# A hybrid diffusion block on one core: the two halves of the retention's gate columns issued ahead of the query convolution instead of behind it

## The chip, the cores and the metric

The kernel runs on one core of one Trainium2 chip. The metric is the device time of one execution in microseconds (us), and a kernel's time is the median of several runs.

## The reference, cut to what matters

One layer of a diffusion backbone with 1024 latent and 256 context tokens of width 1024. One input projection `p = h @ w_in` is split by columns between two groups of four heads. Group A is a gated delta rule (GDN) in both directions, with a centred convolution of five taps on its q, k and v columns. Group B is retention in both directions, with a rotary embedding on q and k, and a gate `rg`:

```
qkv_a, z, ab, rq, rk, rv, rg = jnp.split(p, splits, axis=-1)
qkv_a = concat([short_conv(ctx part, cw), short_conv(latent part, cw)])   # taps, then silu
q, k, v = heads of qkv_a;  q = l2_normalize(q) * HEAD_DIM**-0.5;  k = l2_normalize(k)
...
A   = strict_lower((k * beta) @ k.T * decay)       # per chunk and head
sol = triangular_solve(A + I, [v * beta, k * beta * exp(G)])
qk  = (q @ k.T) * decay
...
o_gdn = rms_norm(o_f + o_b, gdn_norm_g) * silu(z)
o_ret = head_group_norm(r_f + r_b, ret_norm_g) * silu(rg)
y = concat([o_gdn, o_ret])
```

Then follow the output projection, a gated residual, a SwiGLU and a final norm. The columns `rg` are used only in the product `silu(rg)` with the retention's output, long after the part in which they are computed.

## The kernel before

Tokens lie in 10 tiles of 128, tiles 0 and 1 being the context. Products run in two-part fp32: each operand is split into a high part, a copy on ScalarE (L344), and the rest, on VectorE or GpSimd (L345), and three matmuls stand for one.

Two kinds of products fill the stretch around the change. `token_major(g, ...)` computes 256 columns of the projection for a list of tiles, with tokens on partitions: per tile 8 x 3 matmuls of 128x256 (L371 to L373) into a PSUM bank `tm`, a finishing step into `res`, and a store. For the gates (g = 6 and 7, latent tiles alone) that step is a Silu on ScalarE (L532), and the store to DRAM goes out on ScalarE's queue (L387). `conv_block(b, y, lat)` computes one head of 128 columns with channels on partitions, 8 x 3 matmuls for each of two or three pieces of tokens (L611 to L613) into `b2`. Two copies on ScalarE (u, L614, and y, L615), four taps on VectorE (L621) and a Silu (L624) follow.

The program is written in this order: four key heads, each stored and its norms taken (`kstat`); a logarithm and a reciprocal root of the norms; four query heads, each stored to DRAM as `qd` on ScalarE's queue (L682); the gates; then, for the chunks of a batch, `pre(t)` and `invert(b)`, and four value heads. `BATCH = [[0,1,2,9],[3,8,4,7],[5,6]]` lists the tiles of each batch. `pre(t)` loads the keys `kc` and, for a latent tile, the queries `qc` (both on SP, L664), multiplies keys by keys (kk, L705), transposes the queries (qt, L710) and multiplies them by the keys (kq, L715). For each direction it loads a row of decays into `gw` (L718, two buffers), masks it on GpSimd (e, L722), takes its exponential on ScalarE (L726), multiplies on VectorE (ut, L730, and sp, L732) and stores ut as `un` (L733). The second exponential of gw (L735) is multiplied by the queries on GpSimd (L736), which frees that gw. `invert(b)` loads `un` as yr (L751), inverts blocks of 32 on VectorE in 31 steps (L759, L765, L767) and stores them as `xd` (L771). `merge(b)` loads them again (L787, L788) and joins them on PE (m1, L807 on). The value heads are transposed (vT, L856), scaled on ScalarE into vt (L859, two buffers) and stored as `sd` (L860). The gate columns of z, `token_major` of g = 8 and 9, come behind the merges.

That is the order of the text only. A scheduler places each instruction in the order of its engine by the estimated time at which its inputs are ready, with the place in the text as priority, and at run time each engine keeps the order it was given. So products with nothing to wait for stand between those that wait.

Of the kernel before, what the change touches and what calls it, by code (L numbers as in the profile page):

```python
# [38 lines left out]
def build(nc, tc, ap, dbg=None, stop=None, marks=None):  # L39
    root = ExitStack()  # L40
    V, S, G, T, SY = nc.vector, nc.scalar, nc.gpsimd, nc.tensor, nc.sync

    def pool(name, bufs=1, side=None, space=None):
        kw = {}
        if side is not None:
            kw["side"] = side
        if space is not None:
            kw["space"] = space
        if space is not DRAM:
            kw["reuse_waits"] = "tile"  # L50
        es = ExitStack()
        p = es.enter_context(tc.tile_pool(name=name, bufs=bufs, **kw))
        root.push(es)
        p_close[id(p)] = es
        return p
# [10 lines left out]
    def checkpoint(name):  # L66
        if dbg is not None:
            marks.append((name, int(nc.cur_bb.bb.instructions[-1].name.split("-")[-1])))
        if stop == name:
            raise Stop()  # L70
# [120 lines left out]
    try:  # L191
# [40 lines left out]
        W2 = None  # L232
# [127 lines left out]
        def tm_weights(g, kh, pl, q=S):  # L360
            return weights(ap["wt"][g, :, 4 * kh:4 * kh + 4, :], [4, 256], V, pl, q, raws.get((g, kh)), g == 0)

        def tm_bank(g):
            return bank_a("tm")[:, 0:WIDE if g == 0 else 256]

        def tm_half(o, w, kh, t):

            tsl = slice(t * P, (t + 1) * P)
            whi, wlo = w
            for k in range(4 * kh, 4 * kh + 4):  # L370
                T.matmul(o, hhi[:, k, tsl], whi[:, k % 4, :], start=(k == 0), stop=False)  # L371
                T.matmul(o, hhi[:, k, tsl], wlo[:, k % 4, :], start=False, stop=False)  # L372
                T.matmul(o, hlo[:, k, tsl], whi[:, k % 4, :], start=False, stop=(k == KT - 1))  # L373
# [5 lines left out]
        def tm_store(g, t, o, finish, store, pl):  # L379
            early = g < 2  # L380
            res = (W2 if early else R1).tile([P, 256], F32, tag="res", name="res", bufs=4 if early else 2)
            finish(t, o[:, 0:256], res)
            if g == 0:
                S.activation(xa[:, t, :], o[:, 256:WIDE], AF.Copy)
            nm, c0 = GROUPS[g // 2], (g % 2) * 256
            dst = zd[t - 2, :, c0:c0 + 256] if nm == "z" else rd[t, :, RD[nm], c0:c0 + 256]
            store.dma_start(dst, res)  # L387

        def token_major(g, tiles, finish, store, pl, q=S):

            w = [tm_weights(g, kh, pl, q) for kh in range(2)]

            for p in range(0, len(tiles), 2):
                pair = [(t, tm_bank(g)) for t in tiles[p:p + 2]]
                for kh in range(2):
                    for t, o in pair:
                        tm_half(o, w[kh], kh, t)
                for t, o in pair:
                    tm_store(g, t, o, finish, store, pl)
# [47 lines left out]
        W2 = pool("w2", bufs=2)  # L447
# [39 lines left out]
        def ada_rest(c, half):  # L487

            c0 = c * D + half * 512
            src = ap["ada2"][2 * (c - 2) + half]  # L490
            acc = R2.tile([P, 512], F32, tag="acc", name="acc", bufs=1)
            for k in range(KT):
                if k % 2 == 0:
                    w = R2.tile([P, 2, 512], F32, tag="adaw2", name="adaw2", bufs=2)
                    SY.dma_start(w, src[k // 2])
                if k == 0:
                    V.tensor_scalar(acc, w[:, 0], csl[:, k, 0:1], None, ALU.mult)
                else:
                    V.scalar_tensor_tensor(acc, w[:, k % 2], csl[:, k, 0:1], acc, ALU.mult, ALU.add)
            ps = bank_b("gr")  # L500
            if c in (2, 5):
                row = R2.tile([1, 512], F32, tag="row", name="row", bufs=1)
                SY.dma_start(row, ap["adarow"][c0:c0 + 512].unsqueeze(0))
                T.matmul(ps[:1, :], ones[:, 0:1], acc, start=True, stop=True)
                V.tensor_tensor(row, row, ps[:1, :], ALU.add)
                SY.dma_start(grow[0 if c == 2 else 1][:, half * 512:(half + 1) * 512], row)
            else:
                for k in range(4):
                    T.matmul(ps[:, 2 * k:2 * k + 2], acc[:, k * P:(k + 1) * P], ones[:, 0:2], start=True, stop=True)
                ks = slice(half * 4, half * 4 + 4)  # L510
                o = ada2[:, c - 3, ks]
                V.tensor_tensor(o, ps[:, 0:8].rearrange("p (k t) -> p k t", t=2)[:, :, 0],
                                adab[:, 8 * c + 4 * half:8 * c + 4 * half + 4], ALU.add)
                if c == 4:
                    V.scalar_tensor_tensor(o, o, 1.0, gffn[:, ks], ALU.add, ALU.mult)
# [18 lines left out]
        LAT, ALL = list(range(2, TT)), list(range(2, TT)) + [0, 1]  # L534
# [67 lines left out]
        def conv_block(b, y, lat):  # L602

            whi, wlo = weights(ap["wg"][b], [KT, P], G if b % 2 else V, W, SY if b in (4, 5) else S)
            u = CV.tile([P, NTOK], F32, tag="u", name="u", bufs=2)
            for c0, n in (CHUNKS[1:] if lat else CHUNKS):
                ps = bank_c("b2")
                o = ps[:, :n]
                for k in range(KT):
                    hh, hl = hhi[:, k, c0:c0 + n], hlo[:, k, c0:c0 + n]  # L610
                    T.matmul(o, whi[:, k, :], hh, start=(k == 0), stop=False)  # L611
                    T.matmul(o, whi[:, k, :], hl, start=False, stop=False)  # L612
                    T.matmul(o, wlo[:, k, :], hh, start=False, stop=(k == KT - 1))  # L613
                S.activation(u[:, c0:c0 + n], o, AF.Copy)  # L614
                S.activation(y[:, c0:c0 + n], o, AF.Copy, scale=cw[:, b, 2:3])  # L615
            segs = [(NCTX, NLAT)] if lat else [(0, NCTX), (NCTX, NLAT)]
            for i, e in ((0, V), (1, V), (3, V), (4, V)):
                for s0, n in segs:
                    sh = i - 2
                    lo, hi = s0 + max(0, -sh), s0 + n - max(0, sh)  # L620
                    e.scalar_tensor_tensor(y[:, lo:hi], u[:, lo + sh:hi + sh], cw[:, b, i:i + 1], y[:, lo:hi],  # L621
                                           ALU.mult, ALU.add)
            a0 = NCTX if lat else 0
            S.activation(y[:, a0:], y[:, a0:], AF.Silu)  # L624

        def newy():
            return CV.tile([P, NTOK], F32, tag="y", name="y", bufs=3)
# [46 lines left out]
        sv = rsqrt(GS, nkf, TT * H, "sv")  # L674
        V.tensor_tensor(sv, sv, nkf, ALU.mult)
        sv3 = sv.rearrange("p (t h) -> p t h", h=H)
        for h in range(H):
            y = newy()
            conv_block(h, y, True)
            if h < 2:  # L680
                ada_rest(5, h)
            S.dma_start(qd[:, :, h, :].rearrange("t p j -> p t j"),  # L682
                        y[:, NCTX:].rearrange("p (t j) -> p t j", j=P))

        checkpoint("q")
        for g in (6, 7):
            token_major(g, LAT, fin_gate, S, W2, SY)
        checkpoint("rg")
        close(R2)
        close(W2)  # L690
# [964 lines left out]
```

## Time and profile before

| what | before |
|---|---|
| runs, median (lowest to highest) | 1478.84 us (1476.53 to 1480.8), 3 runs |
| the profiled execution | 1477.96 us, its span 1476.2 us |
| granted TensorE clock, mean | 0.983 |
| PE, weight loads, VectorE, ScalarE, GpSimd busy | 95%, 81%, 65%, 42%, 40% |

Names of engines: PE is TensorE's matmul, DVE is VectorE, ACT ScalarE, POOL GpSimd, SP the engine that issues most loads. A row of a timeline has the start, the duration, the engine, the line, the operation, what it writes from what it reads, and a count; in brackets stands the idle time of that engine ahead of it and what ended it. ACTq and SPq are instructions that issue a DMA. A row of a stretch has its window and its length, then the busy time of PE, PE's weight loads, DVE, ACT and POOL with their counts, the granted clock, the share of the DMA engines and GB/s.

### The profile page before, as it was taken

The page shows a single profiled execution, that of the slowest core. Times are in us where ns is not written, and L with a number is a line of the kernel's source. Part 1 is how long each engine was busy: PE and PEld are TensorE (multiplying, and loading weights), DVE is VectorE, ACT ScalarE, POOL GpSimd, SP SyncE. Part 2 cuts the span into 40 slices and gives each one's busy share as a digit, 9 for nine tenths or more (in the row PEclk, how much of TensorE's full clock was granted, in tenths as well). Part 3 has the DMA queues.
Part 4 walks back from the last instruction along what each step waited for, and adds up shares of the span by engine and source line. Part 5 has one row for each costly group of instructions (what it writes and reads, how often), then busy time and mean ns, then how long its engine had stood idle before and what let it go on. Part 6 is the DMA issues. An engine that isn't in the chain of part 4 may idle for free.

```text
span 1476.2 us, 24111 instructions
## 1 busy us (share of the span) xinstructions
PE 1397.2 (95%) x8919; PEld 1199.2 (81%) x8919; DVE 964.6 (65%) x1856; ACT 614.0 (42%) x1326; POOL 590.3 (40%) x501
## 2 busy tenths in 40 slices
PE   7999999986789999899799899999999999999997
PEld 2898888975689999898688688877888888788885
DVE  6566789289792435689676877556555564657477
ACT  5643564587333111245443623233333332444445
POOL 0120010243202344234144688898555552335321
PEclk9999999998899999999899999999999999999999
DMA  9536686688888625996532265674222242776863
GB/s 337 197 105 205 189 249 200 219 264 277 282 216 277 238 76 178 416 341 209 184 125 104 97 238 210 242 264 162 105 97 105 107 151 79 260 260 194 288 216 114
DMA packets 170421, 298.14 MB, mean 202 GB/s; under 512 B 43496, under 2 KB 93880, under 8 KB 165952
## 3 DMA queue, kind: packets, MB, share of 16 engines
q1 hardware_dynamic: 118752, 253.17, 50.2%
q10 hardware_dynamic: 49072, 35.83, 7.8%
q0 software_dynamic: 2480, 7.60, 1.4%
q8 instruction: 70, 1.15, 0.3%
q14 instruction: 47, 0.39, 0.1%
HBM read 206.60 MB, written 89.96 MB: 201 GB/s over the span
## 4 chain that ended last, share of the span: by engine, by line
PE 55%; POOL 6%; DMA 5%; DVE 4%; issue 2%; ACT 2%; SPq 1%; ACTq 0%; POOLq 0%; DVEq 0%
PE ffn L1344 7%; PE ffn L1342 6%; PE ffn L1343 6%; PE fo L1470 4%; PE fo L1469 4%; PE fo L1468 4%; PE tm L371 3%; PE tm L373 3%; PE tm L372 3%; PE op L1203 2%; PE op L1201 2%; PE op L1202 2%; DMA wd<-tw 2%; POOL ws L1315 1%; DMA pk<-sd 1%
## 5 line engine op out<-in xcount | busy, mean ns | idle before, releaser
L371 PE MATMUL tm<-whi,hhi 128*128 128x256 f32 (+1 forms) x704 | 199.5, 287 | 7.7 <-ACT vt L859 3.4
L372 PE MATMUL tm<-wlo,hhi 128*128 128x256 f32 (+1 forms) x704 | 199.3, 285 | 2.4 <-issue 2.0
L373 PE MATMUL tm<-whi,hlo 128*128 128x256 f32 (+1 forms) x704 | 197.7, 285 | 0.0
L371 PEld LDWEIGHTS tm<-whi,hhi 128*128 128x128 f32 x704 | 132.8, 190 | 11.8 <-ACT vt L859 3.6
L1342 PE MATMUL ffn<-t,whi 128*128 128x512 f32 x352 | 136.9, 390 | 1.3 <-ACT whi L344 1.3
L1344 PE MATMUL ffn<-t,wlo 128*128 128x512 f32 x352 | 137.0, 390 | 1.0 <-DVE wlo L345 1.0
L1343 PE MATMUL ffn<-t,whi 128*128 128x512 f32 x352 | 137.0, 389 | 0.0
L372 PEld LDWEIGHTS tm<-wlo,hhi 128*128 128x128 f32 x704 | 133.7, 190 | 2.1 <-issue 0.9
L373 PEld LDWEIGHTS tm<-whi,hlo 128*128 128x128 f32 x704 | 132.8, 190 | 2.6 <-issue 1.8
L344 ACT ACTIVATE whi<-wraw 128x512 fp32r<-128x512 f32 (+2 forms) x98 | 75.1, 771 | 141.4 <-PE ffn L1343 80.5
L344 ACT ACTIVATE whi<-ws 128x512 fp32r<-128x512 f32 x88 | 55.6, 632 | 171.5 <-PE ffn L1343 123.4
L345 DVE TENSOR_TENSOR wlo<-ws,whi 128x512 fp32r<-128x512 f32 x88 | 93.9, 1068 | 47.0 <-ACT whi L344 46.8
L1469 PE MATMUL fo<-wlo,ahi 128*128 128x512 f32 x308 | 120.2, 390 | 2.1 <-DVE wlo L345 2.1
L1468 PE MATMUL fo<-whi,ahi 128*128 128x512 f32 x308 | 119.3, 390 | 0.7 <-ACT ahi L344 0.7
L1470 PE MATMUL fo<-whi,alo 128*128 128x512 f32 x308 | 119.0, 390 | 0.0
L345 DVE TENSOR_TENSOR wlo<-wraw,whi 128x512 fp32r<-128x512 f32 (+2 forms) x92 | 99.4, 1082 | 24.6 <-ACT whi L344 24.6
L1342 PE MATMUL ffn<-b,whi 128*128 128x512 f32 x264 | 103.8, 393 | 4.4 <-ACT whi L344 4.4
L1344 PE MATMUL ffn<-b,wlo 128*128 128x512 f32 x264 | 103.6, 393 | 0.8 <-DVE wlo L345 0.8
L1343 PE MATMUL ffn<-b,whi 128*128 128x512 f32 x264 | 103.4, 392 | 0.0
L612 PE MATMUL b<-hlo,whi 128*128 128x512 f32 (+1 forms) x256 | 94.4, 369 | 0.0
L613 PE MATMUL b<-hhi,wlo 128*128 128x512 f32 (+1 forms) x256 | 94.3, 368 | 0.0
L611 PE MATMUL b<-hhi,whi 128*128 128x512 f32 (+1 forms) x256 | 94.3, 368 | 0.0
(446 smaller groups left out, 3448.1 us busy)
## 6 DMA issues: line engine op xcount, KB each, us to landing
adaw<-ada SPq DMA_DIRECT2D x48, 512.0 KB, 4.4
pk<-sd SPq DMA_DIRECT2D x16, 1536.0 KB, 10.0
wraw<-wfi SPq DMA_DIRECT2D x44, 512.0 KB, 3.7
ar<-ad SPq DMA_DIRECT2D x33, 512.0 KB, 4.7
w<-wfo SPq DMA_DIRECT2D x22, 512.0 KB, 5.7
wd<-tw SPq DMA_DIRECT2D x11, 1024.0 KB, 4.8
ad<-act SPq DMA_DIRECT2D x20, 512.0 KB, 3.0
raw<-wd SPq DMA_DIRECT2D x20, 512.0 KB, 4.9
```

Source lines behind the costliest of these rows:

```text
L344: S.activation(hi, raw, AF.Copy)
L345: e.tensor_tensor(lo, raw, hi.bitcast(F32), ALU.subtract)
L371: T.matmul(o, hhi[:, k, tsl], whi[:, k % 4, :], start=(k == 0), stop=False)
L372: T.matmul(o, hhi[:, k, tsl], wlo[:, k % 4, :], start=False, stop=False)
L373: T.matmul(o, hlo[:, k, tsl], whi[:, k % 4, :], start=False, stop=(k == KT - 1))
L612: T.matmul(o, whi[:, k, :], hl, start=False, stop=False)
L1342: T.matmul(o, whi[:, k, :], xhi(xn, slice(0, 4), k), start=(first and k == 0), stop=False, **kw)
L1343: T.matmul(o, whi[:, k, :], xlo(xn, slice(0, 4), k), start=False, stop=False, **kw)
L1344: T.matmul(o, wlo[:, k, :], xhi(xn, slice(0, 4), k), start=False, stop=(k == 3), **kw)
L1468: T.matmul(po[g][i], ahi[:, ts], whi, start=(j == 0 and not kw), stop=False, **kw)
L1469: T.matmul(po[g][i], ahi[:, ts], wlo, start=False, stop=False, **kw)
L1470: T.matmul(po[g][i], alo[:, ts], whi, start=False, stop=(j == FH - 1), **kw)
```

## The change

The loop over the two halves of the gate columns is moved from behind the query heads to ahead of them, behind the last step on the key norms. Nothing else is edited. The lines between the two places get numbers higher by two, so the store of the query head is L682 before and L684 after; the numbers of all other lines named here stay.

```diff
--- before.py
+++ after.py
@@ -674,6 +674,8 @@
         sv = rsqrt(GS, nkf, TT * H, "sv")
         V.tensor_tensor(sv, sv, nkf, ALU.mult)
         sv3 = sv.rearrange("p (t h) -> p t h", h=H)
+        for g in (6, 7):
+            token_major(g, LAT, fin_gate, S, W2, SY)
         for h in range(H):
             y = newy()
             conv_block(h, y, True)
@@ -683,8 +685,6 @@
                         y[:, NCTX:].rearrange("p (t j) -> p t j", j=P))
 
         checkpoint("q")
-        for g in (6, 7):
-            token_major(g, LAT, fin_gate, S, W2, SY)
         checkpoint("rg")
         close(R2)
         close(W2)
```

What the scheduler makes of it shows in the orders. PE first, where the first products of `pre` (kk) stand. In the names, tm_2826 is a bank of the last gate products, b2_3572 the second piece of the first value head, kk_2897 and kk_2930 belong to the context tiles. Before:

```order
L371 MATMUL tm_2826<-whi_2651,hhi_86 128x256
L372 MATMUL tm_2826<-wlo_2652,hhi_86 128x256
L373 MATMUL tm_2826<-whi_2651,hlo_87 128x256
L705 MATMUL kk_2897<-kc_2895 128x128 x4
L705 MATMUL kk_2930<-kc_2928 128x128 x4
L613 MATMUL b2_3572<-hhi_86,wlo_3539 128x512
L611 MATMUL b2_3572<-hhi_86,whi_3538 128x512
```

After, with b2_2848 the second piece of the last query head and b2_3545 the first piece of the first value head:

```order
L611 MATMUL b2_2848<-hhi_86,whi_2814 128x512
L612 MATMUL b2_2848<-hlo_87,whi_2814 128x512
L613 MATMUL b2_2848<-hhi_86,wlo_2815 128x512
L705 MATMUL kk_2897<-kc_2895 128x128 x2
L705 MATMUL kk_2930<-kc_2928 128x128 x4
L611 MATMUL b2_3545<-hhi_86,whi_3538 128x256
```

Before, the last thing ahead of kk is a gate product, and the query head was done 258 rows earlier. Now it is the last query head, and the gates end 176 rows above. Also on PE, the place where the first queries are read (qt_2970, qc_2968). Before, it stands among the products of the first value head (b2_3599):

```order
L612 MATMUL b2_3599<-hlo_87,whi_3538 128x512
L705 MATMUL kk_2963<-kc_2961 128x128 x4
L710 MATMUL qt_2970<-ident_65,qc_2968 128x128 x4
L613 MATMUL b2_3599<-hhi_86,wlo_3539 128x512
L611 MATMUL b2_3599<-hhi_86,whi_3538 128x512
```

After, it stands behind all of the first value head and 22 of 24 products of the first piece of the second (b2_3672):

```order
L612 MATMUL b2_3672<-hlo_87,whi_3665 128x256
L613 MATMUL b2_3672<-hhi_86,wlo_3666 128x256
L611 MATMUL b2_3672<-hhi_86,whi_3665 128x256
L710 MATMUL qt_2970<-ident_65,qc_2968 128x128 x4
L715 MATMUL kq_2979<-qc_2968,kc_2961 128x128 x4
L705 MATMUL kk_3022<-kc_3020 128x128 x4
```

On ACT, the place of the last query head's Silu and store, y_2341 before and y_2813 after. The e are the exponentials of L726, e_2986 and e_3004 those of the first tile with queries. Before, it stands among the gates:

```order
L614 ACTIVATE u_3544<-b2_3545 128x256
L615 ACTIVATE y_3537<-b2_3545,cw_1293 128x256
L624 ACTIVATE y_2341<-y_2341 128x1024
L532 ACTIVATE res_2707<-tm_2657 128x256
L682 DMA qd_1297<-y_2341 128x8x128
L387 DMA rd_115<-res_2707 128x256
```

After:

```order
L726 ACTIVATE e_2950<-e_2950,nG_1284 128x128 x4
L726 ACTIVATE e_2986<-e_2986,nG_1284 128x128 x4
L735 ACTIVATE gw_2984<-gw_2984 128x512
L624 ACT_TABLE_LOAD
L624 ACTIVATE y_2813<-y_2813 128x1024
L726 ACT_TABLE_LOAD
L726 ACTIVATE e_3004<-e_3004,nG_1284 128x128 x4
L735 ACTIVATE gw_3002<-gw_3002 128x512
L614 ACTIVATE u_3544<-b2_3572 128x512
L615 ACTIVATE y_3537<-b2_3572,cw_1293 128x512
L684 DMA qd_1297<-y_2813 128x8x128
```

The Silu and the store now stand among the exponentials, with table loads between, and the store behind both exponentials of the first tile with queries.

The third place, on ACT too, is the last value head (y_3918, its copies vt_4019, vt_4028 and vt_4039) against tile 6, the last of `pre` (e_4137 and e_4155, its two directions). Before:

```order
L726 ACTIVATE e_4137<-e_4137,nG_1284 128x128 x3
L735 ACTIVATE gw_4135<-gw_4135 128x512
L712 ACTIVATE qt_4121,nq_1292<-qt_4121 128x128
L726 ACTIVATE e_4155<-e_4155,nG_1284 128x128 x4
L735 ACTIVATE gw_4153<-gw_4153 128x512
L712 ACTIVATE qt_4121,nq_1292<-qt_4121 128x128
L624 ACT_TABLE_LOAD
L624 ACTIVATE y_3918<-y_3918 128x1280
L859 ACTIVATE vt_4019<-vT_4016,svy_2076 128x128 x2
```

After:

```order
L624 ACT_TABLE_LOAD
L624 ACTIVATE y_3918<-y_3918 128x1280
L712 ACTIVATE qt_4121,nq_1292<-qt_4121 128x128 x2
L859 ACTIVATE vt_4019<-vT_4016,svy_2076 128x128 x2
```

```order
L859 ACTIVATE vt_4028<-vT_4023,svy_2076 128x128 x4
L387 DMA zd_116<-res_5018 128x256
L859 ACTIVATE vt_4039<-vT_4034,svy_2076 128x128 x4
L726 ACT_TABLE_LOAD
L726 ACTIVATE e_4155<-e_4155,nG_1284 128x128
L860 DMA sd_1296<-vt_4028 128x4x128
L726 ACTIVATE e_4155<-e_4155,nG_1284 128x128 x3
```

The Silu stood behind both directions of tile 6. Now it stands ahead of both, and e_4155 stands behind the third copy vt_4039.

## The prediction

> **What bounds the kernel now.** I read the page's head first, then the busy time in stretches of 40 us around the change, then the timeline of PE, and last those of the engines that PE was seen to wait for.
>
> ```profile
> span 1476.2 us, 24111 instructions
> PE 1397.2 (95%) x8919; PEld 1199.2 (81%) x8919; DVE 964.6 (65%) x1856; ACT 614.0 (42%) x1326; POOL 590.3 (40%) x501
> 240.00:280.00 40.00, 40.00 (x299) 37.45 (x298) 21.01 (x41) 17.73 (x34) 6.80 (x9) 1.00 0.54 166
> 280.00:320.00 40.00, 38.17 (x232) 32.86 (x231) 25.93 (x33) 31.94 (x94) 15.26 (x14) 1.00 0.89 282
> 320.00:360.00 40.00, 31.54 (x186) 26.77 (x184) 39.48 (x60) 34.40 (x92) 18.73 (x16) 0.97 0.82 255
> 360.00:400.00 40.00, 25.56 (x188) 24.97 (x189) 31.38 (x68) 16.23 (x52) 10.02 (x8) 0.81 0.88 297
> 400.00:440.00 40.00, 34.45 (x891) 32.55 (x889) 37.02 (x97) 11.94 (x21) 0.95 (x1) 0.96 0.87 204
> ```
>
> TensorE is busy 95% of the span, so a move can pay or cost only where PE stands still. In the stretch rows PE comes first, then weight loads, DVE, ACT, POOL, the clock, the DMA share. PE has no gap up to 280 us, where convolutions and gates run. From 280 to 440 it lacks 30 us of work (1.8, 8.5, 14.4, 5.5), and in 320 to 360 DVE is full (39.48 of 40). After that PE is full again with projection columns as filler, so the end of the program moves by what the sum of PE's gaps before then moves. The gates keep PE covered while the last query head travels to DRAM and back. The move takes that cover and puts value convolution there.
>
> ```profile
> 276.17 0.28 PE L373 MATMUL tm<-whi,hlo 128*128 128x256 f32 x1
> 276.29 1.39 PE L705 MATMUL kk<-kc 128*128 128x128 f32 x11
> 283.18 0.39 PE L611 MATMUL b<-hhi,whi 128*128 128x512 f32 x1
> 283.40 0.39 PE L612 MATMUL b<-hlo,whi 128*128 128x512 f32 x1
> 283.64 1.05 PE L705 MATMUL kk<-kc 128*128 128x128 f32 x8
> 284.52 0.60 PE L710 MATMUL qt<-ident,qc 128*128 128x128 f32 x4
> ...
> 361.79 2.05 PE L705 MATMUL kk<-kc 128*128 128x128 f32 x8 [6.72 <-issue]
> 375.06 2.39 PE L856 MATMUL vT<-ident,y 128*128 128x128 f32 x10 [9.27 <-ACT y L624]
> 387.02 0.39 PE L371 MATMUL tm<-whi,hhi 128*128 128x256 f32 x1 [3.38 <-ACT vt L859]
> ```
>
> The first kk follows the last gate product without a gap. The three gaps that matter are 6.72, 9.27 and 3.38 us, in brackets. The 9.27 us end with the Silu of the last value head.
>
> **What is removed and added.** No arithmetic changes: the same 2 x 8 x 24 gate products, their Silus (L532) and stores (L387), and the weight loads, which keep their rows on SP. Until the query convolution PE had no gap in 240 to 280 us and the gates' weights are asked for as early as before: I cost that part at 0. PE work is its cover, and without it one weight load's landing of some 5 us would be the price. On ACT the Exp of the decay (L726) now alternates with the Silu of the query head (L624), and the program holds 26 table loads where it held 20.
>
> **The query head's round trip.** This is the moved dependence, and each of its steps is repriced.
>
> ```profile
> 257.17 1.06 ACT L624 ACTIVATE y<-y 128x1024 f32<-128x1024 f32 x1 [6.29 <-DVE y L621]
> 258.26 0.38 ACTq L682 DMA_DIRECT2D qd<-y  x1
> DMA to landing us min/median/max: 3.2/5.3/6.3
> 264.41 0.90 SPq L664 DMA_DIRECT2D qc<-qd  x2
> DMA to landing us min/median/max: 4.7/5.6/6.3
> ```
>
> The first landing row is that of the tile qd (this store), the second that of qc (this reload). Before, qd is stored at 258.26, qc asked for at 264.41, and PE reads it at 284.52: 14 us of slack behind a landing of 5.6.
>
> Now PE's order: ahead of the last half of the first kk stand the same products as before less 35 of the value convolution, 24 of 256 columns (276.17 to 276.29: 0.12 us each) and 11 of 512 (283.18 to 283.40: 0.22), that is 2.9 + 2.4 = 5.3 us. So the query convolution ends near 276.3 - 5.3 = 271 instead of 243. Behind it, up to the reading of q (L710), stand 46 products of 256 columns and 48 of 512, and two and a half groups of kk of 0.9 us (283.64 to 284.52): 5.5 + 10.6 + 2.2 = 18.3, so PE is at the reading of q at 290.
>
> ```profile
> 279.62 0.91 SPq L718 DMA_DIRECT2D gw<-grow_d  x2
> 286.90 1.27 ACT L726 ACTIVATE e<-e,nG 128x128 f32<-128x128 f32 x4
> 288.08 0.62 ACT L735 ACTIVATE gw<-gw 128x512 f32<-128x512 f32 x1
> 288.40 0.32 SPq L718 DMA_DIRECT2D gw<-grow_d  x1
> L736 POOL TENSOR_TENSOR sp<-gw,qc x16: 1264/1299/2011, 287.1 to 372.7; 128x512 f32<-128x512 f32 x16
> 372.44 1.28 ACT L624 ACT_TABLE_LOAD   x1
> 373.73 1.27 ACT L624 ACTIVATE y<-y 128x1280 f32<-128x1280 f32 x1
> ```
>
> When does ACT get to the store of qd? In its order it now stands behind both Exp groups of the first tile with a query and the second gw (L735), which ended at 288.08 + 0.62 = 288.7. These hang on kk, which comes 5 us earlier, so 283.7; among them now stand the Silu (1.06) and three table loads (1.28 each): 283.7 + 1.06 + 3.84 = 288.6, say 288. If the taps alone decided it would be near 284. A landing of 3.2 to 5.3 gives 291 to 294, the reload another 4.7 to 5.6: q is there between 296 and 299, I take 298. PE arrives at 290, so a new gap of some 8 us, 6 with the short landings; before there was none here.
>
> On the table load the Trainium skill, "ScalarE: Activation LUTs", What ACT_TABLE_LOAD costs, gives 1.28 us for the load and 1.38 us of drain, 2.66 in all. The trace agrees with the load (372.44, 1.28) and shows no drain behind it (the Silu starts at 373.73, 0.01 us after the load's end). By the page the store of qd would come 3 x 1.38 = 4 us later and the whole would be some 1488 to 1490 us; with 0.01 us on record it gets no chance of its own.
>
> **What the late q delays.** On SP the reload of q now stands right ahead of the third gw load with queries (it was sent 24 us before it), and that load needs a buffer that the POOL product with q (L736, 1.30 us) frees. Before, that load went out at 288.40, right behind POOL's first product (287.1 + 1.3). Now q at 298 + 1.3 gives 299.5: 11 us late. A part is absorbed because DVE stood in the way there:
>
> ```profile
> 295.48 4.10 DVE L621 SCALAR_TENSOR_TENSOR y<-u,cw,y 128x1023 f32<-128x1023 f32 x4
> 300.71 0.69 DVE L730 TENSOR_TENSOR ut<-kk,e 128x512 f32<-128x512 f32 x1 [1.13 <-issue]
> 311.99 1.47 DVE L759 COPY L<-yr 64x1024 f32<-64x1024 f32 x1
> ```
>
> The batch's last ut (300.71) waited behind 4.1 us of value taps that were done first. So of 11 us 8 to 9 reach it, and with it the load of yr and the start of the first inversion (L759, 311.99): now 320.5. I take +8.5, between 0 (everything hidden) and 11.
>
> **What stands behind it.** From there DVE is the bound until the last value head's taps are done:
>
> ```profile
> 367.40 0.39 DVE L767 TENSOR_TENSOR X<-X,tmp 128x231 f32<-128x231 f32 x1
> 369.74 0.69 DVE L730 TENSOR_TENSOR ut<-kk,e 128x512 f32<-128x512 f32 x1 [1.95 <-ACT e L726]
> 370.34 1.27 DVE L621 SCALAR_TENSOR_TENSOR y<-u,cw,y 128x1022 f32<-128x1022 f32 x1
> 385.83 1.14 ACT L859 ACTIVATE vt<-vT,svy 128x128 f32<-128x128 f32 x4 [7.78 <-DMA sd<-vt]
> 376.44 9.31 DMA sd<-vt
> 381.00 1.40 SPq L771 DMA_DIRECT2D xd<-X  x2
> 403.89 3.41 SPq L787 DMA_DIRECT2D U<-xd  x4
> ```
>
> It took 370.34 + 1.27 - 311.99 = 59.6 us. In the new order the last tap stands ahead of tile 6's ut and of two steps of the inversion that were before it: 1.95 of idle, the ut (0.6 from 369.74 to 370.34) and twice 0.35 (as at 367.40) go, so 56.4 remain. 320.5 + 56.4 = 377, and the Silu takes 1.3 (its table can be loaded while it waits), so PE gets its vT at 378.5, 3.5 later than 375.06. The gate products z behind it, which wait for the vt copies, shift by the same 3.5, from 387.02 to 390.5. That is PE's first term: **+3.5**.
>
> The second comes from ACT's order. The Exp of tile 6's second direction (e_4155) used to stand ahead of the last Silu; now it stands behind the third vt copy, which waits until the first vt store has landed (7.78 us of wait, the landing 9.31). With the shift of 3.5 that copy ends at 385.83 + 1.14 + 3.5 = 390.5, then a table load and Exp (2.6): DVE gets its ut at 393, its last steps of the inversion end near 395, where before the result was stored at 381.00: +14. From there it is 23 us of stores, loads and reloads (381.00 to 403.89) until the first merge product can run: 418 instead of 404. PE meanwhile has 17.2 us of z gates as before (387.02 to 404.2) and 46 more gate products now standing ahead of the merge (5.4 us): until 390.5 + 17.2 + 5.4 = 413. So a gap of 5 takes the place of the present 1.35 there: **+3.5 to +4**. The later inversions follow 9 to 14 us late, but PE has filler behind each; their small gaps (2 us together) I leave as they are, within 2 either way. Sum: +7 to +8 on the profiled 1477.96 us (span 1476.2 and 1.8 around it) gives 1485.3; that execution lies 0.9 below the median 1478.84, so I say **1486**.
>
> **The rivals.**
> Hidden after all: the store goes out at 284 (taps decide), both landings are short (3.2 and 4.7): q is there at 292.2, PE waits 2 us, the gw load is at 294 (+5), of which DVE's 4.1 us of taps swallow most. Then the chain of L759 moves by 2, vT by -3, z gates by -3; the late e_4155 still costs 5 to 7 in the first merge: between -2 and +4, 1477 to 1483. For it speaks that PE has 30 us of gaps in this region that can take a new one's place; against it that DVE is full in 320 to 360.
>
> Faster: the last value head's Silu no longer waits for tile 6, which takes 3.2 us from DVE's way and about 2 of Exp and table load from ACT's (371.6, the tap's end, to 373.73). If q is not late, vT stands at 312 + 56.4 + 1.3 = 369.7 and PE gains 5: 1473 to 1474. This decides when L759 starts by about 313; what speaks for it is the bracket of 9.27 us, against it that reading q follows only 19 us behind the convolution's end, where the way through DRAM alone took 26 (258.26 to 284.52, with slack).
>
> The tail isn't absorbed: e_4155's 14 us go through merge 0 and the two that follow in full, PE's filler having been used up earlier as cover for q. +13 to +16: 1491 to 1495. For it speaks that value convolution, now spent ahead of 290, is missing between 311 and 388 us.
>
> **How the numbers follow.** A difference below 0.3% (4.4 us) is about what a measurement of this kernel can tell from none. The forecast (+4.5 to +11) gets 0.45, the tail not absorbed 0.13, hidden 0.26, faster 0.16. Faster counts to below -0.3% for nearly all of its chance, and some of hidden's low end: 0.17; hidden and the forecast's low end: 0.27; the rest 0.56. The range from 1474 (faster's own) to 1496 leaves out the outer ends of both tails.
>
> **What would show it.** Right: ACT's store of qd near 288, the first qt on PE near 298 with a gap of 6 to 9 us ahead, a gw load near 299.5, L759 near 320; the vT gap ends near 378, tile 6's last ut behind the last vt copy, the first merge product near 418. Wrong: a qt without a gap, L759 by 313, or a vT before 372; or gate weights late near 200, which would put a gap where PE had none.

## The result, and the profile after

The changed kernel takes 1498.3 us (1497.95 to 1499.65, 4 runs) against 1479.76 us before: a ratio of 1.0131, with a 95% interval of 1.0113 to 1.0149. That is 18.5 us slower. The forecast was slower, by 7 us, and its range ended at 1496.

The page of the changed kernel, its span and the busy time of each engine:

```profile
span 1496.3 us, 24112 instructions
PE 1408.5 (94%) x8919; PEld 1209.5 (81%) x8919; DVE 973.0 (65%) x1856; ACT 622.5 (42%) x1332; POOL 596.9 (40%) x501
```

The span grew by 20.1 us (one execution each). PE ran the same 8919 matmuls, and in this pair they took 11.3 us longer (1408.5 against 1397.2); the other 8.8 us are new idle time. The split belongs to these two executions and not to the kernels: the profiled execution before had a mean granted clock of 0.983, while 56 other executions of the same kernel had 0.974 to 0.985, on average 0.979. The changed kernel's four had 0.973 to 0.977, on average 0.975. By these averages the slower clock makes some 5 us of the loss (an estimate: 0.0034 of 1480 us). Some of the difference is also older than the change. PE starts the first projection columns (L371), long ahead of the moved loop, at 39.89 us against 38.42, because the clock of the first 40 us was 0.91 in this execution and 1.00 in the one before. So PE came 1.5 us late to the change already. The stretches of 40 us show where it lost the rest:

```profile
320.00:360.00 40.00, 34.77 (x189) 29.70 (x187) 39.22 (x61) 30.05 (x85) 18.73 (x13) 0.95 0.82 275
360.00:400.00 40.00, 31.37 (x217) 30.71 (x218) 33.30 (x65) 30.27 (x74) 11.93 (x12) 0.83 0.78 229
400.00:440.00 40.00, 25.81 (x482) 23.83 (x481) 27.68 (x72) 9.05 (x16) 1.81 (x1) 0.79 0.86 231
440.00:480.00 40.00, 32.11 (x681) 29.84 (x682) 21.52 (x53) 10.51 (x18) 3.63 (x7) 0.96 0.75 221
```

From 320 to 400 us PE is busier than before (34.77 and 31.37 where it had 31.54 and 25.56). The loss begins behind that: 25.81 busy in 400 to 440 against 34.45, at a clock of 0.79 against 0.96. The timeline of PE names the gaps, in brackets with what ended them:

```profile
376.64 2.37 PE L856 MATMUL vT<-ident,y 128*128 128x128 f32 x10 [2.44 <-ACT y L624]
383.24 0.39 PE L371 MATMUL tm<-whi,hhi 128*128 128x256 f32 x1 [0.83 <-ACT res L532]
410.65 0.28 PE L807 MATMUL m<-t,U 32*32 32x32 f32 x2 [3.95 <-DMA t<-xd]
415.84 0.58 PE L371 MATMUL tm<-whi,hhi 128*128 128x256 f32 x1 [4.91 <-ACT whi L344]
419.74 1.73 PE L807 MATMUL m<-t,U 32*32 32x32 f32 x122
427.76 0.18 PE L814 MATMUL m<-U,xt 32*32 32x32 f32 x1 [3.26 <-DMA U<-xd]
```

The same stages before, on SP, PE and VectorE:

```profile
375.45 0.51 SPq L783 DMA_DIRECT2D U<-un  x1
404.21 0.58 PE L807 MATMUL m<-t,U 32*32 32x32 f32 x4
406.46 1.48 PE L807 MATMUL m<-t,U 32*32 32x32 f32 x124
410.66 0.21 PE L814 MATMUL m<-U,xt 32*32 32x32 f32 x1
415.24 1.09 DVE L769 COPY XT<-X 128x1024 f32<-128x1024 f32 x1
```

The last value head's transposes come at 376.64, 1.6 us later than before. The z gates behind them go on after their first pause at 383.24, earlier than before (387.02). Then the first merge waits: its first product starts at 410.65 (404.21 before), and its second step, the first to need what is loaded from `xd` into U, at 427.76 (410.66 before). SP's timeline has the loads for it:

```profile
389.87 0.52 SPq L771 DMA_DIRECT2D xd<-X  x1
...
395.56 1.70 SPq L783 DMA_DIRECT2D U<-un  x1
397.37 0.90 SPq L872 DMA_DIRECT2D rope<-rope  x1
399.46 10.69 SPq L788 DMA_DIRECT2D t<-xd  x4
410.32 2.60 SPq L751 DMA_DIRECT2D yr<-un  x4
412.96 0.62 SPq L783 DMA_DIRECT2D U<-un  x1
413.62 13.01 SPq L787 DMA_DIRECT2D U<-xd  x4
```

Before, the loads of yr for the third batch went out ahead of t, U followed t at once (403.89, in 3.41 us), and the second batch's load of 2 MB (U from un) had left at 375.45. Now yr and that load stand between t and U, and U takes 13.01 us to issue. Meanwhile ScalarE is held at a store of the z gates, PE waits 4.91 us for the weight split (L344) behind that store, and VectorE waits for the same split in the middle of the second inversion:

```profile
413.72 0.34 ACTq L387 DMA_DIRECT2D zd<-res  x1
414.73 1.06 ACT L344 ACTIVATE whi<-wraw 128x1024 fp32r<-128x1024 f32 x1 [12.81 <-issue]
415.82 1.23 DVE L345 TENSOR_TENSOR wlo<-wraw,whi 128x1024 fp32r<-128x1024 f32 x1 [9.02 <-ACT whi L344]
```

The store's data had been ready since 401.9. What it waited for is a count. Each DMA raises one when it lands; the program gives the DMAs of SP and ScalarE eight such counts in turn, and a DMA may not go out before the last one with its count has landed. The store shares its count with the first load of yr for the third batch, which SP had sent only at 410.32, behind all four t loads. In the trace that count's last step comes at 413.64, and the store goes out at 413.72.

The hold moves PE too. The first merge's first step has 122 of its 128 products behind the gate products that waited for these weights, so it ends at 421.5 (407.9 before). Of the second step's lateness of 17.1 us only the last 3.26 are a wait for U alone.

The second inversion ends at 429.73 instead of 415.24, and the merges behind it end at 495.5 instead of 473.5. From there to the end the difference stays between 17 and 23 us.

### The profile page after: what moved, and what is told of

Its sections match the earlier page's. It is cut to its first block, busy times and chain, and to the rows that moved or that the text cites. A ratio compares the mean times of both kernels' runs of the same rounds, so it can differ in the third digit from the quotient of the medians.

```text
span 1496.3 us, 24112 instructions
## 1 busy us (share of the span) xinstructions
PE 1408.5 (94%) x8919; PEld 1209.5 (81%) x8919; DVE 973.0 (65%) x1856; ACT 622.5 (42%) x1332; POOL 596.9 (40%) x501
## 4 chain that ended last, share of the span: by engine, by line
PE 52%; POOL 7%; DVE 5%; DMA 5%; issue 3%; ACT 2%; SPq 1%; ACTq 0%; POOLq 0%; DVEq 0%
PE ffn L1344 6%; PE ffn L1343 6%; PE ffn L1342 6%; PE fo L1468 5%; PE fo L1470 5%; PE fo L1469 5%; PE tm L372 2%; PE tm L373 2%; PE tm L371 2%; PE op L1201 2%; PE op L1203 2%; PE op L1202 2%; POOL ws L1315 1%; DMA wd<-tw 1%; PE up L929 1%
## 5 line engine op out<-in xcount | busy, mean ns | idle before, releaser
L371 PE MATMUL tm<-whi,hhi 128*128 128x256 f32 (+1 forms) x704 | 200.5, 289 | 9.5 <-ACT whi L344 5.7
L371 PEld LDWEIGHTS tm<-whi,hhi 128*128 128x128 f32 x704 | 133.7, 191 | 12.5 <-ACT whi L344 6.1
L344 ACT ACTIVATE whi<-wraw 128x512 fp32r<-128x512 f32 (+2 forms) x98 | 75.1, 772 | 162.2 <-PE ffn L1343 79.1
L344 ACT ACTIVATE whi<-ws 128x512 fp32r<-128x512 f32 x88 | 55.6, 632 | 172.7 <-PE ffn L1343 120.0
```

The lines of the kernel that those rows point to most:

```text
L344: S.activation(hi, raw, AF.Copy)
```

## The experiments

Fourteen kernels were run. Each edit of the program also moves rows elsewhere, since the scheduler places everything anew; so for each the moments at which the stages start are read from its trace, not only its time. Two executions also differ by themselves: e12, whose time is that of the kernel before, has the last value head's transposes at 378.53 and the end of the merges at 477.4, where the profile before has 375.06 and 473.5. So a shift of less than 4 us between two profiles shows nothing alone. "Changed" is the kernel with the gates first, "before" the one with the gates behind the query heads.

| run | made from | median us | ratio to before (95%) |
|---|---|---|---|
| e1_inv2_first | changed | 1491.2 | 1.0040 to 1.0088 |
| e2_zstore_pool | changed | 1494.18 | 1.0070 to 1.0105 |
| e3_zsplit_pool | changed | 1494.01 | 1.0059 to 1.0110 |
| e4_late_q | before | 1488.11 | 1.0036 to 1.0070 |
| e5_after_tail | changed | 1496.87 | 1.0094 to 1.0140 |
| e6_before_tail | before | 1484.14 | 1.0020 to 1.0059 |
| e7_half | one half moved | 1486.07 | 1.0027 to 1.0056 |
| e8_gates_last | gates last | 1492.92 | 1.0078 to 1.0110 |
| e9_u1_late | changed | 1499.45 | 1.0096 to 1.0165 |
| e10_u1_late_pre | changed | 1495.43 | 1.0080 to 1.0126 |
| e11_late_q_rope | before | 1487.28 | 1.0031 to 1.0066 |
| e12_rope_pool | before | 1479.61 | 0.9973 to 1.0006 |
| e13_after_gw4 | changed | 1486.24 | 1.0030 to 1.0060 |
| e14_before_gw4 | before | 1483.07 | 1.0012 to 1.0047 |

**Three edits of the tail, one at a time.**

```diff
 e1:  -        merge(0)
      -        SY.dma_start(rope, ap["rope"])
               invert(2)
      +        merge(0)
      +        SY.dma_start(rope, ap["rope"])
 e2:  -            token_major(g, LAT, fin_gate, S, W)      # g = 8, 9
      +            token_major(g, LAT, fin_gate, G, W)
 e3:  -  weights(ap["wt"][g, ...], [4, 256], V, pl, q, ...)
      +  weights(ap["wt"][g, ...], [4, 256], G if g in (8, 9) else V, pl, q, ...)
```

> The changed kernel with one edit in the text: invert(2) stands ahead of merge(0), so that the four loads of yr for the third batch go out on SP ahead of the first merge's t loads, as in the kernel before, instead of between its t and U loads. Theory A (the time is lost behind 380 us, where the first merge's two kinds of loads come apart and ScalarE and VectorE are held up behind them): U of the first merge lands by about 421 instead of 427.8, and the time falls by 5 to 10 us, to 1488 to 1493. Theory B (the late query alone; all later stages are only carried along): within 4 us of 1498.

> The changed kernel with the stores of the z gates issued on GpSimd's queue instead of ScalarE's. Theory A: ScalarE is no longer held at a store from 402 to 413.7, the weight split behind it (L344, at 414.7) comes at about 402, VectorE's 9.0 us of idle ahead of L345 go, and the second inversion ends near 420 instead of 429.5: 5 to 10 us faster, 1488 to 1493. Theory B: the second inversion is not on the path, within 4 us of 1498.

> The changed kernel with the low part of the z gates' weights (L345) on GpSimd instead of VectorE; ScalarE stays held at its store. Theory A: VectorE no longer waits 9.0 us in the middle of the second inversion, which ends near 420; PE still waits for the weights (4.91 us). 4 to 8 us faster, 1490 to 1494. Theory B: within 4 us of 1498.

Medians of 1491.2, 1494.18 and 1494.01: 7, 4 and 4 us below the changed kernel, so the tail does hold time that can be won, as theory A had it. But e1 did not do it in the way that was expected. Its yr went out ahead of t, and still U arrived late:

```profile
426.61 0.18 PE L814 MATMUL m<-U,xt 32*32 32x32 f32 x1 [2.57 <-DMA U<-xd]
```

The second step of the first merge is at 426.61, not at 421. The gain came later: its second merge starts at 445.7 instead of 451.3. In e2 and e3 the second inversion ended at 423.6 and 423.2 instead of 429.7, some two thirds of what was expected (e3's profile is of its fastest execution, 1489.3). In e2, with the stores off ScalarE's queue, the weights came in time and the merge's first step was done by 416.7; its second step then waited for U alone:

```profile
428.29 0.23 PE L814 MATMUL m<-U,xt 32*32 32x32 f32 x1 [7.67 <-DMA U<-xd]
```

**The late query alone.** In the kernel before, only the last query head is made late.

```diff
-            S.dma_start(qd[:, :, h, :].rearrange("t p j -> p t j"),
-                        y[:, NCTX:].rearrange("p (t j) -> p t j", j=P))
+            if h < 3: S.dma_start(...)                      # the same store, for heads 0 to 2
         for g in (6, 7):
-            token_major(g, LAT, fin_gate, S, W2, SY)
+            last = token_major(g, LAT, fin_gate, S, W2, SY)
+        one = GS.tile([P, 1], F32, tag="one", name="one")
+        V.tensor_scalar(one, last[:, 0:1], 0.0, 1.0, ALU.mult, ALU.add)
+        S.activation(y[:, NCTX:], y[:, NCTX:], AF.Copy, scale=one[:, 0:1])
+        S.dma_start(qd[:, :, 3, :].rearrange("t p j -> p t j"), y[:, NCTX:].rearrange("p (t j) -> p t j", j=P))
```

> The kernel before, gates in their old place, with the last query head alone made late: its store waits for the last gate result (a copy of the head by a scale of 1 that is worked out from that result), so it goes out near 279 instead of 258 and the query lands near 290 instead of 270. Theory B (the late query makes the loss): PE reaches the query at 284.5, so it comes 5 us late or more, and the kernel takes 1484 to 1495. Theory A: the start of the first inversion moves by some 3 to 5 us, the order behind 380 us stays as before, and it costs 0 to 4 us: 1479 to 1483.

1488.11 us: theory B's range, and the start of the first inversion moves as far as in the changed kernel. But on SP the load of the rotary table waited there, and the first inversion's result behind it:

```profile
400.85 0.33 SPq L880 DMA_DIRECT2D rope<-rope  x1
401.24 1.15 SPq L779 DMA_DIRECT2D xd<-X  x2
```

The inversion had ended at 391.7, its stores went out at 401.24. So e11 took that block away, by issuing the table's load on GpSimd's queue, and e12 is the same edit in the kernel before:

```diff
-        SY.dma_start(rope, ap["rope"])
+        G.dma_start(rope, ap["rope"])
```

> The kernel before with the last query head late, as e4_late_q, and the load of the rotary table on GpSimd's queue: in e4_late_q that load stood ahead of the first inversion's stores on SP and kept them from 391.7 to 401.2. If e4's 9 us came from that block, the stores go out at 392 and the time is 1479 to 1484. If the late query itself costs the 9 us, it stays at 1486 to 1490.

> The control: the kernel before with the rotary table's load on GpSimd's queue and nothing else. In the kernel before, that load goes out at 392.4 between loads that wait for nothing else: within 4 us of 1479 by either theory.

```profile
391.58 1.17 SPq L779 DMA_DIRECT2D xd<-X  x2
393.78 7.78 SPq L779 DMA_DIRECT2D xd<-XT  x2
```

The stores go out at 391.58, as wanted, and the time stays at 1487.28; the control stands at 1479.61. So a late query with the gates left in their place costs 7 to 9 us (with the edit's own copy of the head, 1.16 us on ScalarE), and the block by the table's load was not the cause. That is a good part of the 18.5 us, not all of it.

**Do the tail edits add up?** e5 puts the edits of e1 and e3 together in the changed kernel, e6 in the kernel before.

> The changed kernel with two edits behind 380 us together: invert(2) ahead of merge(0) in the text, and the low part of the z gates' weights on GpSimd. Theory A2 (two losses that add: the late query some 9 us, as the late query alone cost, and the tail some 7 to 10): 1485 to 1490, the late query's 9 us staying. Theory B2 (both edits mend the same wait): no better than 1491, which the first edit alone gave.

> The kernel before with the same two edits, as the control. Theory A2: in the kernel before the first merge's loads already stand together and its ScalarE has the weight split done in time, so there is little to mend: 1475 to 1481. Theory B2 (a general weakness of the tail that the move only lengthened): 5 to 8 us faster, 1471 to 1475.

They don't: 1496.87, where each alone gave 1491 and 1494, and in the kernel before the two edits cost some 5 us (1484.14). Theory A2 fails in both kernels. B2's "no better than 1491" holds for e5, but the gain that it expected in the kernel before did not come. Two edits that were meant to take waits away can make the program slower. Why is not shown: the scheduler built another order around them, and the low part of a weight split takes 2.34 to 2.49 us on GpSimd where VectorE takes 1.22.

**Less of the change, and more of it.**

```diff
 e7:  for g in (6,): token_major(...)     # ahead of the query heads
      for g in (7,): token_major(...)     # behind them
 e8:  -        for g in (6, 7): token_major(g, LAT, fin_gate, S, W2, SY)
      -        for g in (8, 9):
      +        for g in (6, 7, 8, 9):
                   token_major(g, LAT, fin_gate, S, W)
```

> One half (g = 6) ahead of the query heads, the other (g = 7) left behind them: 22 us of gate products keep their place between the query convolution and the reading of q. If the cover is what counts, the last query head is stored by about 268, the query lands before PE asks for it, and the time is that of the kernel before: 1477 to 1483. If any shift of the query heads costs in proportion: about 1488.

> Both halves of the gates behind the merges, beside those of z, so the query heads stay as early as in the kernel before and value convolution alone covers the reading of q. If only the query's lateness counts, q is in time and the kernel is not slower than before: 1474 to 1482. If gate products are needed as cover between 243 and 290 us or value convolution is missed between 311 and 388, PE stands idle there for 20 to 40 us that it can't win back: 1495 to 1520.

With one half moved the last query head is stored at 260.25 and read at 278.32, so the query is early, as the first theory said; but the time is 1486.07, not that of the kernel before. With the gates last, q is read at 268.3 and the merges end at 456.5, 17 us earlier than before; yet the kernel is 14 us slower. So an early query isn't enough. In e8 the whole chain of batches was faster, while the gate products still had to be done behind it; that this makes its loss is read from the order and was not tested.

**The load of 2 MB between t and U.**

```diff
+            if b == 1:
+                V.tensor_copy(uu[:, 0, 0, 0, 0:1], hold0)     # hold0: written from merge 0's first result
             SY.dma_start(uu.rearrange("p e c h j -> p e (c h) j"), un[b])
 e10 besides: pre(5), pre(6) written ahead of the loop over the value heads
```

> The changed kernel with the second batch's big load (U of batch 1 from un1, L783, 2 MB) made to wait for the first merge's first product (one column of U written ahead of the load, from a value that the merge has just worked out), so that it stands behind the first merge's U loads on SP instead of right ahead of them. Theory C (that load, 20 us earlier in the kernel before, is what parts the first merge's t and U loads): the first merge's second product starts at 417 to 420 instead of 427.8, and the time falls to 1489 to 1494. Theory D (the DMA engines are full there, whatever the order): it stays at 425 or later and the time within 3 us of 1498.

> As the run before, and pre of tiles 5 and 6 written ahead of the value heads, which brings the exponential of tile 6's second direction ahead of two of the last value head's three vt copies. If that exponential holds the first inversion (VectorE waits 2.4 and 1.6 us for it in the changed kernel), the inversion ends at 385 to 387 instead of 390 and the time is 2 to 5 us below that of the run before. If not, within 2 us of it.

```profile
412.13 2.60 SPq L753 DMA_DIRECT2D yr<-un  x4
414.77 3.06 SPq L791 DMA_DIRECT2D U<-xd  x4
424.70 0.34 SPq L787 DMA_DIRECT2D U<-un  x1
...
417.32 0.58 PE L371 MATMUL tm<-whi,hhi 128*128 128x256 f32 x1 [4.57 <-ACT whi L344]
421.23 1.91 PE L811 MATMUL m<-t,U 32*32 32x32 f32 x122
426.18 0.21 PE L821 MATMUL m<-U,xt 32*32 32x32 f32 x1
```

The load of 2 MB now stands 10 us behind the merge's own loads (in the kernel before it had left 37 us earlier than in the changed one, not 20), and these go out in 3.06 us instead of 13.01. Still the second step starts at 426.18, and the time is 1499.45. So theory C's forecast fails: this load alone doesn't make the loss. But the run doesn't show that U's lateness costs nothing. U landed by 424.3 here, and no wait for it stands ahead of the product. What was late is the first step: 122 of its products start at 421.23, behind gate products that waited 4.57 us for weights, since ScalarE was held at its store again, until 415.10 (the t load with its count landed at 415.03). Two waits end close together, U's loads and the held weights; e9 takes away the first, e2 the second, and no run takes away both. In e10 the inversion ended at 390.5, not at 385 to 387, the merge's second step came at 421.2 and the time was 1495.43: a little better, for a reason other than the one expected.

**The buffers through which the late query acts.** The loads of the third and fourth gw wait until GpSimd's product with the query frees a buffer. Four buffers take that wait away.

```diff
-                gw = GP.tile([P, H, P], F32, tag="gw", name="gw", bufs=2)
+                gw = GP.tile([P, H, P], F32, tag="gw", name="gw", bufs=4)
-                tmp = GI.tile([P, 256], F32, tag="tmp%d" % b, name="tmp", bufs=2)
+                tmp = GI.tile([P, 256], F32, tag="tmp", name="tmp", bufs=1)
```

> The changed kernel with four buffers for the decay rows gw instead of two (the room comes from one shared tmp buffer in the inversion, which VectorE alone uses in order). The loads of gw for the third and fourth tile of the first batch then stand ahead of the query's reload. Theory E (the late query delays the batch through these buffers, and all the rest follows): the first inversion starts at 308 to 313 instead of 318, its result is stored by 383 instead of 390, and the time falls to 1480 to 1487. Theory F (the order alone): the start moves, but the time stays above 1492.

> The kernel before with the same four buffers, as the control and as a version that could beat both. Its query lands at 270, ahead of its use, but the gw loads still wait for buffers (POOL 49 us in all for gw). Theory E: the first inversion starts 3 to 6 us earlier and the time falls by 0 to 5 us, 1474 to 1479. Theory F: any new order costs, 1482 to 1488.

1486.24 us: with the gates in the new place and four buffers, 12 of the 18.5 us are gone. VectorE's timeline of that run, then SP's:

```profile
316.29 1.04 DVE L759 COPY L<-yr 64x1024 f32<-64x1024 f32 x1 [4.41 <-DMA yr<-un]
...
374.91 0.67 DVE L730 TENSOR_TENSOR ut<-kk,e 128x512 f32<-128x512 f32 x1
383.56 1.12 DVE L769 COPY XT<-X 128x1024 f32<-128x1024 f32 x1
```

```profile
377.05 0.32 SPq L783 DMA_DIRECT2D U<-un  x1
...
399.32 7.63 SPq L788 DMA_DIRECT2D t<-xd  x4
407.00 3.08 SPq L787 DMA_DIRECT2D U<-xd  x4
```

The start of the first inversion moved by 2 us only (316.29; 308 to 313 was expected), so that half of theory E is wrong. What moved is its end: the last ut of tile 6 is at 374.91 instead of 387.93, the inversion ends at 383.56 instead of 389.88, the load of 2 MB leaves at 377.05 as it did before the change, t and U go out together and the merge's second step is at 414.17. In the kernel before, the four buffers brought nothing (1483.07, slower by 0.12 to 0.47%). With four buffers in both kernels the move of the gates costs 1486.24 - 1483.07 = 3 us, with two it costs 18.5; part of the smaller difference is that the kernel before got 4.5 us slower.

That the buffers carry the 12 us isn't shown, only that this edit takes them away. Its new order also has tile 6 ahead of the last Silu again (the last ut at 374.91, the transposes at 376.53) and SP's loads nearly in the sequence of the kernel before, and no run has the one without the other.

No version beat the kernel before.

## Why the prediction was wrong, step by step

**Up to the query: right.** The store of the last query head was forecast for 288, the next gw load for 299.5, the first inversion's start for 320.5.

```profile
288.91 0.37 ACTq L684 DMA_DIRECT2D qd<-y  x1
292.22 0.79 SPq L664 DMA_DIRECT2D qc<-qd  x2
295.74 0.60 PE L710 MATMUL qt<-ident,qc 128*128 128x128 f32 x4
296.18 0.32 SPq L718 DMA_DIRECT2D gw<-grow_d  x1
318.34 1.21 DVE L759 COPY L<-yr 64x1024 f32<-64x1024 f32 x1 [0.26 <-DMA yr<-un]
```

They came at 288.91, 296.18 and 318.34. The reload took 3.5 us and not 5.6, so q was there at 296 rather than 298. The gap of 6 to 9 us ahead of it did not come: PE reached q at 295.74, not at 290. Of these 5.7 us, 1.5 were there before the change, 2.42 are a wait for ScalarE's copy of a bank, late among the exponentials and table loads (the row at 291.61 below), and 1.6 are the half speed behind that wait. The inversion's start moved by 6.3 us, where 8.5 had been taken.

**The first term: too high.** +3.5 for the last value head's transposes; the trace has +1.6 (376.64), of which 1.5 can be older than the change. So the term was next to nothing.

**The second term: mis-sized, and this is the step that failed.** It said: from the inversion's end 23 us to the merge, PE's filler lasts until 413, "so a gap of 5 takes the place of the present 1.35: +3.5 to +4". The inversion ended at 389.9, 8.9 us late, better than the 14 forecast, since the third vt copy hardly waited. And yet, where one gap of 5 us was forecast in place of 1.35, PE had gaps of 1.65, 3.95, 4.91 and 3.26 us between 403 and 428; before, it had 1.35, 0.93 and 1.96 between 404 and 416. That is +9.5 us of waiting where the term says +3.5 to +4, and half-speed matmuls besides. Two things were missing from the term. It followed the merge to its first product (410.65, forecast 418) and not to the rest of its first step nor to the second, which needs U: that is 17 us late. And it counted the z gates as filler until 413 and left out that their second half needs a weight split on ScalarE, which stands in order behind a store (held until 413.72). So PE ran out of filler at 406.7, and VectorE, whose part of the same split stands within the second inversion, stood 9.02 us. Then "the later inversions I leave as they are, within 2 either way" was wrong by 20: the last merge ended 22 us late.

**What no term had: the clock.** "A move can pay or cost only where PE stands still" left out that PE can also run slower, and every gap was priced at its own length. (Nor is PE "full again" behind 440: it is 31.51 us busy in 680 to 720 of the profile before.) The profile after shows what a gap can cost besides:

```profile
291.61 0.58 PE L611 MATMUL b<-hhi,whi 128*128 128x256 f32 x1 [2.42 <-ACT y L615]
291.99 0.42 PE L612 MATMUL b<-hlo,whi 128*128 128x256 f32 x1
...
294.76 0.31 PE L613 MATMUL b<-hhi,wlo 128*128 128x256 f32 x1
294.91 0.28 PE L611 MATMUL b<-hhi,whi 128*128 128x256 f32 x1
295.03 0.28 PE L612 MATMUL b<-hlo,whi 128*128 128x256 f32 x1
415.00:420.00 5.00, 3.73 (x36) 3.15 (x39) 3.98 (x8) 1.17 (x2) 0.00 (x0) 0.50 0.89 367
```

Behind a gap of 2.42 us, matmuls of 256 columns follow each other every 0.21 us until 294.8, then every 0.12: 3.3 us at half speed, 1.6 us lost, on top of the gap. Behind the gap of 4.91 us the clock of the whole stretch 415 to 420 is 0.50. Before, the long gaps stood together (355 to 387); now they are spread from 291 to 428. The price is not a fixed one. At 33 to 35 us both profiles have the same two gaps, of 1.0 and 1.6 us; behind them PE ran at full speed in the execution before and at half speed in the one after. The Trainium skill, "TensorE: Matmul & The Clock Gate", HAM oscillation, warns of this, with idle gaps above some 3.4 us as those to avoid. The trace agrees with the halved speed; it shows it behind a shorter gap of 2.42 us as well. A prediction that priced a new gap of 5 us should have asked what runs behind it. How much of the 18.5 us the clock makes was not tested by a run of its own; the estimate from the averages is some 5.

**The rivals.** The nearest is "the tail isn't absorbed" (13 to 16 us, a chance of 0.13): the first merge's lateness was passed on in full. Its reason was another. The inversion was 8.9 us late and not 14, and PE's filler wasn't used up as cover for q: gate products were there, but their weights weren't. So it came near in part by luck. "Hidden after all" and "faster" are out: the last value head's Silu did come ahead of tile 6, but PE gained nothing by it.

**What stays open.** The late query alone costs 7 to 9 us (e4, e11), and 12 of the 18.5 go with four gw buffers and the order that comes with them (e13). How the loss divides between the lateness and the order can't be told by these runs: edits of the tail moved the time by 5 to 7 us, for better in e1 and for worse in e6. Whether U's loads and the held weights, taken away together, would win back the tail is open too. In e1 the load of 2 MB still stood right ahead of U's loads (411.46), and these took 13.07 us to issue; why one such load can take SP 5 us to issue is not shown.

## What to carry to other kernels

When independent work is moved to another place, ask which wait it covered there, and follow the late result through the buffers that it holds: here an edit to four buffers in place of two went with two thirds of the loss. Follow a delay through every step of the stage, not to its first product, and ask of each DMA which earlier one it has to wait for and what stands in order behind it, on every engine. A new TensorE gap can cost half-speed matmuls besides; and before a difference between two single profiles is read, compare their clocks and a stage ahead of the change.

## What the runs showed of the hardware that was not expected

A gap of 2.42 us on PE was followed by 3.3 us of matmuls at half speed (0.21 against 0.12 us); after gaps of 1.0 and 1.6 us one execution ran at half speed and another did not. A store on ScalarE's queue, its data ready at 401.9, went out at 413.72, when an unrelated load on SP with the same count had landed (413.64); in e9 the same store went out at 415.10, behind a landing at 415.03. And a table load on ScalarE costs 1.28 us and no more: at 285.04 it starts 0.02 us behind the instruction ahead of it, and the Silu starts at 286.33.

```profile
284.41 0.61 ACT L735 ACTIVATE gw<-gw 128x512 f32<-128x512 f32 x1
285.04 1.28 ACT L624 ACT_TABLE_LOAD   x1
286.33 1.06 ACT L624 ACTIVATE y<-y 128x1024 f32<-128x1024 f32 x1
```
